# A two-layer diffusion backbone on one core: the last third of a modulation matrix-vector product moves from the gMLP stage to the mixer's output projection

## The chip, the core and the metric

The program runs on 1 core of one Trainium2 chip. The metric is the device time of one execution in microseconds (us). TensorE (PE) multiplies matrices into PSUM, VectorE (DVE), ScalarE (ACT) and GpSimd (POOL) work element by element, and SyncE (SP) issues the DMAs, in program order: a DMA whose buffer is not free holds back those behind it on SP.

## The reference

The model has an even layer (gMLP beside a bidirectional long convolution, "Hyena") and an odd one (attention). Each layer has a SwiGLU feed-forward part, and each sub-layer is modulated by six vectors per layer, which come from one product with a conditioning vector:

```python
def adaln(cond, w_mod, b_mod):
    return jnp.split(jax.nn.silu(cond) @ w_mod + b_mod, 6, axis=-1)

sh1, sc1, g1, sh2, sc2, g2 = adaln(c[:, None, :], mod_w[layer], mod_b[layer])
h = modulate(x, norm1_g[layer], sh1, sc1)
y = gmlp_hyena_mixer(h, ...)          # even layer; ends with concatenate([y_a, z]) @ w_out
x = x + g1 * y
x = x + g2 * swiglu(modulate(x, norm2_g[layer], sh2, sc2), ffn_w_gu[layer], ffn_w_down[layer])
```

There are 512 latent and 256 context tokens (six tiles of 128), and 1024 features; `mod_w` is 1024 by 6144 for each layer. Everything is float32.

## The kernel before

**Stages.** `build` runs the filters of the convolution, then the gMLP stage (`gmlp`), the convolutions (`hyena`), the mixer's output projection (`mix_out`), the first feed-forward part, attention and the second feed-forward part. A tile scheduler sets the order on every engine from the order of the code, priorities and its own estimates; a matmul with 3-way split operands (`mm3`, and `prod` in `project_tm`) is three matmuls, high by high, low by high, high by low.

**Weight loads and fill steps.** Every block of weights goes through `wload` (L158): a DMA of 512 KB into a tile `raw`, a rounding copy to `whi` on ACT (L166), and the remainder `wlo` on DVE (L167). `load_y` (L700) does the same with the mixer's activations, from `yu` (gMLP) and `yz` (convolution) in DRAM, 384 KB each. All of them, and the modulation too, share three `raw` buffers: a new `raw` can be loaded when an earlier one has been read for the last time.

Before each load, `wload` and `load_y` call `fill`, which takes `nfill` (or one) steps from a generator `self.filler`. The generator is `adaln` (L320): for a layer and one of three groups of 2048 columns it makes 16 steps; a step loads 512 KB of `mod_w` into a `raw` and multiplies it by the conditioning columns `sc` in four matmul instructions (eight records in the trace), straight from `raw`, into one PSUM tile `pa`. A 17th step adds the bias, transposes the result and stores it to `moddr`. The pool `pa` has one buffer, and the long convolutions use it as well, for the sums of their inverse transforms (L771). Group 1 holds the gate of the mixer and the shift of the feed-forward part, group 2 its scale and gate; group 2 is first needed by the norm ahead of the feed-forward part.

**gMLP stage.** `gmlp` has 16 weight loads (eight in two `project_tm`, eight in four `wcols`). `nfill` is 2 there, so the 32 loading steps of groups 1 and 2 all stand in this stage; the scheduler starts the first of them while the filters still run. `fill(99)` at L238 takes what is left.

**Mixer's output projection.** `mix_out` (L910) multiplies 16 blocks of 128 activations rows (eight `yu`, eight `yz`) by `even_w_out`, in two halves of the columns, `cg` 0 and 1. A half has eight weight loads; a block of one load is 36 matmuls (six token tiles, two rows of blocks, three products). In half 0 the blocks 0 to 3 use `yu`, which `hyena` has loaded before the last convolutions; the blocks 4 to 7 each load two `yz` tiles first. The tokens' old values `xr` (six DMAs of 512 KB) and the gates (two) are loaded here too. Blocks of half 0 run in between the matmuls of the last two convolutions, which are a chain over PE, DVE, POOL and ACT. The last convolution's result is stored by L800, on SP.

Of the kernel before, what the change touches and what calls it, by code (L numbers as in the profile page):

```python
# [113 lines left out]
class Builder:  # L114
# [93 lines left out]
    def build(self, upto=99):  # L208
        nc, tc = self.nc, self.tc
        with ExitStack() as es:  # L210
            self.base = es.enter_context(self.pool("base"))

            edge = es.enter_context(self.pool("edge", "right"))
            edge.tile([P, EDGE // 4], F32, tag="edge", name="edge", bufs=1)
            self.dr = es.enter_context(tc.tile_pool(name="dr", bufs=1, space=bass.MemoryType.DRAM))
            es.enter_context(self.weights(3, 3, 3))
            e1 = es.enter_context(ExitStack())
            with ExitStack() as e2:
                hp = e2.enter_context(self.pool("hT0", "right"))
                with self.psum(), self.pool("filt") as fp, self.pool("filtc") as fc:  # L220
                    with tc.high_priority(offset=2 * HF):
                        self.consts()
                        self.conditioning()
                        self.filter_hidden(fp)
                    self.prologue()
                    with self.pool("xin", "right") as xp:
                        self.filter_spectra(fc, xp, hp)
                if upto <= 3:
                    return
                e1.enter_context(self.psum())  # L230
                self.filler = self.adaln_steps([(0, 1), (0, 2)])
                with self.pool("gmlp") as gp:
                    self.nfill = 2
                    self.gmlp(gp)
                    self.nfill = 1
                pg0 = e2.enter_context(self.pool("pages0", "right"))
                with self.pool("pages1", "right") as pg, self.pool("conv") as cp:
                    self.fill(99)  # L238
                    self.load_dft(pg)
                    ysu = self.hyena(cp, (pg0, pg), hp)  # L240
                if upto <= 4:
                    return
                self.fill(99)
                xp = es.enter_context(self.pool("xres"))
                xs = [self.t(xp, [P, D], F32, "xr", TT) for _ in range(TT)]
                self.sp = es.enter_context(self.pool("norm"))
                with self.pool("mix") as m2, self.pool("ysz") as mp:
                    self.mix_out(m2, mp, pg0, xs, ysu)
            if upto <= 6:
                return  # L250
            e3 = es.enter_context(ExitStack())
            with self.pool("hT", "right") as hp:
                self.filler = self.adaln_steps([(1, 0), (1, 1), (1, 2)])
                self.ffn(hp, xs, 0)
                self.fill(99)
                if upto <= 7:
                    return
                kvp = e3.enter_context(self.pool("attkv"))
                kv = self.attention_in(hp, kvp, xs)
            e1.close()  # L260
            with self.pool("atts") as ap:
                self.attention(ap, xs[0:4], *kv)
                if upto <= 8:
                    return
            e3.close()
            es.enter_context(self.psum())
            hp = es.enter_context(self.pool("hT2", "right"))
            self.ffn(hp, xs[0:4], 1)
# [913 lines left out]
```

## Time and profile before

| | us |
|---|---|
| median of 3 runs | 2102.85 |
| lowest and highest | 2101.89, 2104.19 |
| the profiled execution | 2103.87 |
| its span in the trace | 2102.1 |
| PE busy in the span | 2006.0 |
| DVE, ACT, POOL busy | 1136.0, 674.4, 281.6 |

The trace is of one execution. "Busy" adds up the records of an engine; idle time in front of an instruction is put down to the engine or DMA that ended it. The granted clock of PE is a share of full speed: 1.00 is 2.4 GHz and half of it the lower level, 1.2 GHz; a mean between the two is a stretch with both.

### The profile page before, as it was taken

What the parts mean: (1) busy time and instruction counts of PE and PEld (TensorE: products, weight loads), DVE (VectorE), ACT (ScalarE), POOL (GpSimd) and SP (SyncE); (2) the same over time, 40 slices, a digit from 0 to 9 for tenths busy, and PEclk for the clock granted to TensorE, in tenths of its full rate; (3) what the DMA queues carried; (4) which work ended last, traced back from release to release, by engine and by line L of the source; (5) the groups of instructions that cost most, each with busy time, mean ns of one, the idle gap of its engine ahead of it and who ended that gap; (6) DMA issues with size and microseconds to landing.
All of it is one profiled execution on the core that took longest, in us unless ns stands there. A gap on an engine that the chain in (4) does not pass through costs nothing.

```text
span 2102.1 us, 28261 instructions
## 1 busy us (share of the span) xinstructions
PE 2006.0 (95%) x11259; PEld 1721.0 (82%) x11259; DVE 1136.0 (54%) x1963; ACT 674.4 (32%) x1234; POOL 281.6 (13%) x267
## 2 busy tenths in 40 slices
PE   5899999999999899899999999998989989999997
PEld 2667878899999788698888888997869978888886
DVE  5876173577787742533333333356677654444447
ACT  4654122333323321511111111213567642222222
POOL 3464000012121210200000000003150020000001
PEclk9999999999999999899999999999999999999999
DMA  7764345522322352333334343221220023233331
GB/s 255 226 213 149 107 152 175 184 78 70 100 83 72 124 203 68 111 91 106 119 107 122 120 121 101 61 69 58 64 80 1 31 71 91 81 110 100 90 106 65
DMA packets 207181, 227.82 MB, mean 108 GB/s; under 512 B 8569, under 2 KB 173546, under 8 KB 206794
## 3 DMA queue, kind: packets, MB, share of 16 engines
q1 hardware_dynamic: 206576, 219.95, 33.5%
q0 software_dynamic: 288, 5.90, 0.7%
q8 instruction: 89, 1.46, 0.3%
q14 instruction: 42, 0.34, 0.1%
q10 hardware_dynamic: 186, 0.17, 0.0%
HBM read 204.91 MB, written 21.07 MB: 108 GB/s over the span
## 4 chain that ended last, share of the span: by engine, by line
PE 88%; DMA 5%; DVE 3%; issue 1%; ACT 1%; POOL 1%; SPq 0%; DVEq 0%; POOLq 0%; ACTq 0%
PE pp L144 16%; PE pp L148 15%; PE pp L146 15%; PE pc L980 13%; PE pp L815 11%; PE pc L815 4%; PE pa L332 2%; DMA raw<-in_mod_w 2%; PE pc L144 1%; PE pc L146 1%; PE pc L148 1%; PE pa L148 1%; PE pa L146 1%; PE pa L144 1%; PE pt L1031 1%
## 5 line engine op out<-in xcount | busy, mean ns | idle before, releaser
L166 ACT CAST whi<-raw 128x1024 fp32r<-128x1024 f32 x208 | 216.7, 1052 | 881.0 <-PE pp L146 279.5
L167 DVE TENSOR_TENSOR wlo<-raw,whi 128x1024 fp32r<-128x1024 f32 x208 | 260.4, 1260 | 374.4 <-ACT whi L166 370.8
L144 PE MATMUL pp<-hTh,whi 128*128 128x384 f32 (+2 forms) x1088 | 324.9, 351 | 1.2 <-ACT whi L166 1.2
L146 PE MATMUL pp<-hTl,whi 128*128 128x384 f32 (+2 forms) x1088 | 324.0, 349 | 0.0
L148 PE MATMUL pp<-hTh,wlo 128*128 128x384 f32 (+2 forms) x1088 | 323.2, 350 | 0.0
L984 DVE TENSOR_TENSOR fy<-pc,fy 128x512 f32<-128x512 f32 x180 | 120.8, 689 | 192.3 <-PE pc L980 192.1
L144 PEld LDWEIGHTS pp<-hTh,whi 128*128 128x128 f32 x1088 | 198.9, 189 | 24.5 <-ACT fa L965 4.9
L148 PEld LDWEIGHTS pp<-hTh,wlo 128*128 128x128 f32 x1088 | 200.0, 189 | 17.2 <-DVE wlo L167 2.1
L146 PEld LDWEIGHTS pp<-hTl,whi 128*128 128x128 f32 x1088 | 199.8, 189 | 12.6
L980 PE MATMUL pc<-whi,fasl 128*128 128x512 f32 x440 | 172.3, 392 | 0.2 <-DVE fasl L155 0.2
L980 PE MATMUL pc<-wlo,fash 128*128 128x512 f32 x440 | 172.2, 391 | 0.0
L908 POOL TENSOR_TENSOR xr<-xr,nh 128x512 f32<-128x512 f32 x35 | 49.1, 1428 | 909.8 <-DVE nh L907 905.7
L980 PE MATMUL pc<-whi,fash 128*128 128x512 f32 x440 | 166.4, 394 | 0.0
L144 PE MATMUL pp<-hT,whi 128*128 128x512 f32 (+1 forms) x512 | 135.7, 341 | 1.3 <-ACT whi L166 1.3
L146 PE MATMUL pp<-hT,whi 128*128 128x512 f32 (+1 forms) x512 | 136.6, 341 | 0.0
L148 PE MATMUL pp<-hT,wlo 128*128 128x512 f32 (+1 forms) x512 | 134.5, 340 | 0.0
L980 PEld LDWEIGHTS pc<-whi,fash 128*128 128x128 f32 x440 | 81.9, 188 | 22.0 <-issue 5.4
L980 PEld LDWEIGHTS pc<-wlo,fash 128*128 128x128 f32 x440 | 82.6, 188 | 17.5
L980 PEld LDWEIGHTS pc<-whi,fasl 128*128 128x128 f32 x440 | 82.6, 188 | 16.3 <-DVE fasl L155 0.6
L144 PEld LDWEIGHTS pp<-hT,whi 128*128 128x128 f32 x512 | 79.5, 189 | 13.6 <-ACT whi L166 1.8
L146 PEld LDWEIGHTS pp<-hT,whi 128*128 128x128 f32 x512 | 80.2, 189 | 10.9
L148 PEld LDWEIGHTS pp<-hT,wlo 128*128 128x128 f32 x512 | 79.7, 188 | 11.5 <-issue 1.2
(344 smaller groups left out, 3794.8 us busy)
## 6 DMA issues: line engine op xcount, KB each, us to landing
raw<-in_mod_w SPq DMA_DIRECT2D x96, 512.0 KB
raw<-in_ffn_w_gu SPq DMA_DIRECT2D x88, 512.0 KB
raw<-in_ffn_w_down SPq DMA_DIRECT2D x44, 512.0 KB
raw<-in_even_w_in SPq DMA_DIRECT2D x40, 512.0 KB
G<-G SPq DMA_DIRECT2D x48, 256.0 KB
Gc<-G SPq DMA_DIRECT2D x16, 768.0 KB
raw<-in_even_w_out SPq DMA_DIRECT2D x16, 512.0 KB
dec<-in_k_dec SPq DMA_DIRECT2D x48, 128.0 KB
```

The lines of the kernel that those rows point to most:

```text
L144: mm(o, lh, rh, start=start, stop=False)
L146: mm(o, lh, rl, start=False, stop=False)
L148: mm(o, ll, rh, start=False, stop=stop)
L166: self.nc.scalar.copy(hi, raw)
L167: self.nc.vector.tensor_sub(lo, raw, hi.bitcast(F32))
L332: nc.tensor.matmul(ps[32 * j:32 * j + 32, hs], self.sc[:, k, :], raw[:, j, :], start=k == 0, stop=k == KT - 1, tile_position=(0, 32 * j))
L815: self.nc.tensor.matmul(ps, x[:, ts], y[:, a, :], start=k + a == 0 and i == 0, stop=k + a == wk - 1 and i == 2)
L908: (eng or nc.gpsimd).tensor_add(x[:, cs], x[:, cs], tmp)
L980: nc.tensor.matmul(ps, x[:, ts], y[:, 0, cs], start=i == 0 and j == 0, stop=i == 1 and j == 2)
L984: nc.vector.tensor_add(ys[q][:, cs], ps, ys[q][:, cs])
L1031: self.nc.tensor.transpose(ps[:, js], src[:, js], self.eye)
```

## The change

The generator for the gMLP stage holds group 1 alone and gives one step per weight load. Group 2 gets a generator of its own in `mix_out`, which is drained when `mix_out` ends; `fill` in `wload` and `load_y` takes one step from it per load, so 16 of the 24 loads of `mix_out` have a loading step ahead of them, and one has the closing step.

```diff
-                self.filler = self.adaln_steps([(0, 1), (0, 2)])
+                self.filler = self.adaln_steps([(0, 1)])
                 with self.pool("gmlp") as gp:
-                    self.nfill = 2
                     self.gmlp(gp)
-                    self.nfill = 1
...
-                self.fill(99)
                 xp = es.enter_context(self.pool("xres"))
...
                 with self.pool("mix") as m2, self.pool("ysz") as mp:
+                    self.filler = self.adaln_steps([(0, 2)])
                     self.mix_out(m2, mp, pg0, xs, ysu)
+                    self.fill(99)
```

The lines of the file move up by one from here on (L814 is the old L815, L331 the old L332). In the rows below a number behind a name tells instances apart: `raw_7736` is one load, and its high part is `whi_7738`; `hT_...` are the loaded `yu`, `page` and `ysz` the loaded `yz`.

SP, from the last load of `yu` to the gates of `mix_out`. Before:

```order
L705 DMA raw_7090<-yu_660_2380 128x768
L163 DMA raw_7736<-in_even_w_out 128x2x512
L163 DMA raw_7778<-in_even_w_out 128x2x512
L163 DMA raw_7820<-in_even_w_out 128x2x512
L163 DMA raw_7862<-in_even_w_out 128x2x512
L715 DMA Gc_7540<-G_25_116 128x1536
L163 DMA raw_7904<-in_even_w_out 128x2x512
L705 DMA raw_7910<-yz_662_2382 128x768
L705 DMA raw_7917<-yz_663_2383 128x768
L163 DMA raw_7954<-in_even_w_out 128x2x512
L800 DMA yz_668_2388<-zf_7342 128x768
```

SP, the same place, after:

```order
L704 DMA raw_6979<-yu_660_2380 128x768
L329 DMA raw_7626<-in_mod_w 128x4x256
L163 DMA raw_7632<-in_even_w_out 128x2x512
L329 DMA raw_7674<-in_mod_w 128x4x256
L714 DMA Gc_7429<-G_25_116 128x1536
L163 DMA raw_7680<-in_even_w_out 128x2x512
L329 DMA raw_7722<-in_mod_w 128x4x256
L799 DMA yz_668_2388<-zf_7231 128x768
L799 DMA yz_669_2389<-zf_7529 128x768
L163 DMA raw_7728<-in_even_w_out 128x2x512
L329 DMA raw_7770<-in_mod_w 128x4x256
```

Ahead of the store of the second last convolution there were six weight loads and two of `yz`; now there are two weight loads and three of `mod_w`, and the third weight load stands behind the store of the last convolution (`yz_669`) too.

PE, the end of the last convolution (`pa`) and what follows it. Before:

```order
L148 MATMUL pa_7668<-kd_3752,Yi1l_7665 128x128
L815 MATMUL pp_7733<-whi_7864,hT_7061 128x512
L815 MATMUL pp_7733<-wlo_7865,hT_7060 128x512
L815 MATMUL pc_7734<-whi_7864,hT_7060 128x512
L815 MATMUL pc_7734<-whi_7864,hT_7061 128x512
```

PE, the same place, after:

```order
L148 MATMUL pa_7557<-kd_3641,Yi1l_7554 128x128
L331 MATMUL pa_7625<-raw_7626,sc_92 32x256 x4
L331 MATMUL pa_7625<-raw_7674,sc_92 32x256 x4
L331 MATMUL pa_7625<-raw_7722,sc_92 32x256 x4
L814 MATMUL pp_7619<-whi_7730,hT_6947 128x512
L814 MATMUL pp_7619<-whi_7730,hT_6948 128x512
```

Before, PE goes on with the fourth weight block (`whi_7864`); after, it takes the first three steps of group 2, and then the third block (`whi_7730`, the load `raw_7728`).

SP, in the blocks of half 0 that load `yz`. Before:

```order
L705 DMA raw_8010<-yz_666_2386 128x768
L800 DMA yz_669_2389<-zf_7640 128x768
L898 DMA gate_1595_7726<-moddr_8_99 128x1024
L898 DMA gate_1596_7728<-moddr_8_99 128x1024
L928 DMA xr_7695<-in_x 128x1024
L928 DMA xr_7696<-in_x 128x1024
L705 DMA raw_8017<-yz_667_2387 128x768
L928 DMA xr_7697<-in_x 128x1024
L163 DMA raw_8054<-in_even_w_out 128x2x512
```

SP, the same blocks, after:

```order
L329 DMA raw_7886<-in_mod_w 128x4x256
L163 DMA raw_7892<-in_even_w_out 128x2x512
L329 DMA raw_7898<-in_mod_w 128x4x256
L704 DMA raw_7904<-yz_664_2384 128x768
L329 DMA raw_7911<-in_mod_w 128x4x256
L704 DMA raw_7917<-yz_665_2385 128x768
L329 DMA raw_7954<-in_mod_w 128x4x256
L163 DMA raw_7960<-in_even_w_out 128x2x512
```

A block there took three loads through the `raw` buffers and now takes six, every other one a step of group 2.

## Rows read from the trace of the kernel before

**Rows 1.** The page's busy time of the engines in the whole span, with the share of the span and the number of instructions.

```profile
PE 2006.0 (95%) x11259; PEld 1721.0 (82%) x11259; DVE 1136.0 (54%) x1963; ACT 674.4 (32%) x1234; POOL 281.6 (13%) x267
```

**Rows 2.** Busy time by stretch (from:to, length, busy us and instructions of each engine, granted clock, DMA share, GB/s): the gMLP stage, two stretches of the last convolutions, the rest of half 0, half 1, and the start of the feed-forward part.

```profile
195.00:284.00 89.00, 84.64 (x418) 66.53 (x417) 26.07 (x45) 18.41 (x28) 2.17 (x4) 0.96 0.35 113
284.00:420.00 136.00, 134.66 (x906) 115.02 (x906) 73.14 (x108) 34.10 (x51) 6.92 (x9) 1.00 0.54 182
...
691.49:735.66 44.17, 38.06 (x217) 33.67 (x217) 31.17 (x61) 11.66 (x21) 10.96 (x9) 0.88 0.31 105
735.66:753.06 17.40, 17.40 (x96) 15.04 (x95) 10.97 (x17) 6.32 (x9) 4.60 (x4) 1.00 0.30 91
753.06:789.15 36.09, 36.09 (x161) 29.87 (x161) 13.89 (x18) 8.64 (x11) 5.36 (x5) 1.00 0.73 252
789.15:854.43 65.28, 65.28 (x290) 53.78 (x291) 18.36 (x28) 12.91 (x17) 11.37 (x11) 1.00 0.21 63
...
857.00:910.00 53.00, 44.72 (x265) 39.89 (x264) 24.56 (x48) 24.46 (x48) 1.96 (x3) 0.87 0.42 130
```

**Rows 3.** What PE waited for, of the filters' last 75 us (first two rows) and of the gMLP stage (the others): us in total, times, longest.

```profile
PE pa L332 <- DMA raw<-in_mod_w: 2.7, 2, 2.0
...
PE pp L815 <- DVE G L636: 2.3, 1, 2.3
PE pa L332 <- DMA raw<-in_mod_w: 2.1, 1, 2.1
...
PE pp L144 <- ACT whi L166: 1.3, 1, 1.3
```

**Rows 4.** The chain that ended last (start, us, what), where it runs over three steps of the modulation in one piece; 24 records are three steps.

```profile
331.80 1.43 PE pa L332 x24
```

**Rows 5.** The chain at the gMLP stage's start, where DVE waits for a store of `G` (start, us, what), and PE's timeline there.

```profile
203.86 4.55 DMA G<-G
...
204.78 0.28 PE L148 MATMUL pp<-hfsh,kf 128*128 128x256 f32 x1
207.12 0.64 PE L332 MATMUL pa<-raw,sc 128*32 128x256 f32 x8 [2.06 <-DMA raw<-in_mod_w]
210.06 1.19 PE L815 MATMUL pp<-whi,hT 128*128 128x512 f32 x2 [2.29 <-DVE G L636]
211.05 0.63 PE L815 MATMUL pp<-wlo,hT 128*128 128x512 f32 x1
211.47 1.05 PE L815 MATMUL pp<-whi,hT 128*128 128x512 f32 x2
```

**Rows 6.** Busy time of L815 alone (the mixer's matmuls) by stretch: PE busy, with the records in brackets (one that straddles a border counts in both), weight loads, granted clock, DMA share, GB/s.

```profile
691.49:735.66 44.17, 18.79 (x73) 14.05 (x73) 0.88 0.31 105
735.66:753.06 17.40, 13.73 (x58) 10.63 (x59) 1.00 0.30 91
753.06:789.15 36.09, 36.09 (x159) 29.87 (x160) 1.00 0.73 252
789.15:854.43 65.28, 65.28 (x288) 53.70 (x287) 1.00 0.21 63
```

**Rows 7.** Timelines of the last convolution (start, us, engine, line, idle before): its last `Yi0l` on DVE; PE's last matmuls of the first sum and of the second; ACT's and DVE's reading of the second sum; SP's store of the result.

```profile
740.16 0.75 DVE L155 TENSOR_TENSOR Yi0l<-T,Yi0h 128x512 fp32r<-128x512 f32 x1 [0.41 <-ACT Yi0h L154]
...
745.05 0.28 PE L148 MATMUL pa<-kd,Yi0l 128*128 128x256 f32 x1
...
752.95 0.28 PE L148 MATMUL pa<-kd,Yi1l 128*128 128x128 f32 x1
...
753.32 0.27 ACT L781 COPY B<-pa 128x128 f32<-128x128 f32 x1 [4.74 <-PE pa L148]
...
753.82 0.28 DVE L785 TENSOR_TENSOR s<-pa,B 128x128 f32<-128x128 f32 x1
...
754.65 0.32 SPq L800 DMA_DIRECT2D yz<-zf  x1
```

**Rows 8.** Timelines of ACT at the first two weight blocks of the mixer, and of PE at the first.

```profile
692.18 1.04 ACT L166 CAST whi<-raw 128x1024 fp32r<-128x1024 f32 x1 [0.72 <-DMA raw<-in_even_w_out]
...
698.76 1.05 ACT L166 CAST whi<-raw 128x1024 fp32r<-128x1024 f32 x1 [0.86 <-DMA raw<-in_even_w_out]
...
693.28 2.93 PE L815 MATMUL pp<-whi,hT 128*128 128x512 f32 x6 [1.79 <-ACT whi L166]
```

**Rows 9.** The chain ahead of the first feed-forward part, where it runs over loads of `mod_w` from issue to landing (start, us, what).

```profile
856.63 3.60 DMA raw<-in_mod_w
...
864.76 5.97 DMA raw<-in_mod_w
871.91 4.46 DMA raw<-in_mod_w
```

**Rows 10.** One load of `yz`: SP's issue of the first of two, and ACT's cast that waited for it.

```profile
743.72 3.52 SPq L705 DMA_DIRECT2D raw<-yz  x2
...
746.79 0.84 ACT L707 CAST page<-raw 128x768 fp32r<-128x768 f32 x1 [0.99 <-DMA raw<-yz]
```

**Rows 11.** The tile `raw` from 680 to 860 us: what reads it (ns min/median/max).

```profile
L166 ACT CAST whi<-raw x18: 1037/1054/1057, 692.2 to 853.2; 128x1024 fp32r<-128x1024 f32 x18
L167 DVE TENSOR_TENSOR wlo<-raw,whi x18: 1214/1225/2380, 695.9 to 854.3; 128x1024 fp32r<-128x1024 f32 x18
...
L707 ACT CAST ysz<-raw x5: 832/835/835, 757.3 to 775.1; 128x768 fp32r<-128x768 f32 x5
L708 DVE TENSOR_TENSOR ysz<-raw,ysz x5: 951/959/960, 758.5 to 776.0; 128x768 fp32r<-128x768 f32 x5
```

## The prediction

> **What bounds the kernel now.** I read the engines' busy time first: PE is busy 95% of the span [rows 1], so time is saved only by taking matmuls or PE's waits away, and lost by making PE wait. Then the stages that the change touches, by stretch [rows 2]. The gMLP stage has 4.4 us of PE idle time in 89.0 (195 to 284) and 1.3 in 136.0 (284 to 420). Of the mixer's output projection, the stretch to 735.66 has 6.1 us idle in 44.17; the last 17.40 us of the convolutions, the rest of half 0 (36.09) and half 1 (65.28) have no idle time at all, at full clock. So the place that gives work up has few waits, and the place that receives it has none: what counts is whether it stays so. The waits themselves are the next view [rows 3]: 2.7 us for `mod_w` in the filters, 2.1 for `mod_w`, 2.3 for DVE and 1.3 for a weight block in the gMLP stage.
>
> **The moved work itself: 0.** Three steps take 1.43 us of PE in one piece [rows 4], so a step is 0.48 and the 16 steps are 7.6 us. They leave the filters and the gMLP stage and come back in `mix_out`, where no PE time is free for them: net nothing. The 16 loads of 512 KB move along. The closing step (bias loads, transposes, stores to `moddr`) is moved too; on SP it stands in half 1, with three of its weight blocks loaded ahead, and I cost it at nothing; uncovered it would be one load's time, 4 to 6 us [rows 9].
>
> **Removed waits: -3.0 us.** With one step per load the gMLP stage asks for half the `mod_w`. Of the waits of [rows 3] the one of 2.7, and the 1.3 for a weight block, can go, 4.0 in all. The pair around 207 I leave: the chain there is a store of `G` of 4.55 us that DVE waits for, and PE idles 2.06 and 2.29 in its course [rows 5]; the steps only fill that gap. I take 3.0 of the 4.0, as a load may still land late in the filters. Bounds 0 and -6.4: the lower one has all 4.0 and the 2.4 that the low clock behind the gap costs (twelve matmuls of L815 take 5.1 us from 210.06 instead of 12 x 0.2267 = 2.7; 0.2267 is 65.28 us by 288 records in [rows 6]).
>
> **A. The convolutions' tail: +3.5 us.** `pa` has one buffer, which the convolutions' sums hold, so no step of group 2 can run before the last sum has been read. But their loads are issued earlier, and the order of SP shows three `mod_w` tiles among the first loads; of three `raw` buffers they keep two and then all. So only two weight blocks get through instead of nearly four: 72 mixer matmuls to hide the convolution chain behind, where there were 73 + 58 - 1 = 130 [rows 6]. 58 x 0.2267 = 13.2 us of cover are gone. If the chain were the bound already, PE would idle for all of it: +13.2; if the chain gets faster by as much, since its matmuls no longer queue behind mixer matmuls, 0. Nearer to which? For the last order (17.40 us, PE never idle) I add up the chain alone, from 735.66: 5.25 us to the end of the last `Yi0l` at 740.91; the first sum's matmuls behind it, which ended at 745.33, 4.42 later with mixer matmuls among them, and for which I take 3.05 without; 1.3 until `pa` has been read and can hold the second sum; 1.35 for that sum's last twelve matmuls: 11.0 us [rows 7]. The 3.05, the 1.3 (0.96 as in B, and a wait for PE to take up) and the 1.35 are estimates. PE's work left there is the convolution's 3.67 (17.40 - 13.73) with some transposes, 4.25, and 24 mixer matmuls, 5.4: 9.7. So 1.3 us idle. In the stretch before, the first weight block is now the second load on SP behind a `mod_w`, so its cast comes later, between 692.18 and 698.76 as the second's did [rows 8]; PE waited 1.79 us for the first already, and I take 2.2 more. 1.3 + 2.2 = 3.5.
>
> **B. The gap behind the last convolution: +8.3 us.** The third weight block stands on SP behind the store of the last convolution, and needs a `raw` that the first step gives free only when `pa` has been read. Before, PE went straight on. Now: ACT's copy to DVE's sum takes `pa` away at 754.10, about 0.96 us behind the last matmul, and the store is issued at 754.65 [rows 7]. Then the weight load is issued some 2.0 us behind the last matmul, lands after 4.46 (the middle one of 3.60, 4.46 and 5.97, all loads of the same 512 KB [rows 9]) and is cast in 1.05 [rows 11]: `whi` is ready 7.4 us after the last matmul. PE has three steps, to 0.96 + 1.43 = 2.4. It idles 0.96 + 5.0 = 5.96. Behind the idle stretch of [rows 5] the next twelve matmuls ran at the low clock, 2.4 us longer; I add that here: 8.3. Bounds 5 (landing in 3.60, clock kept) and 10 (5.97).
>
> **C. The ring of `raw` buffers: +8.5 us.** Blocks 4 to 7 of half 0 each took three loads; now six: three `mod_w`, one weight block, two `yz`. PE's work for a block is 36 x 0.2267 + 3 x 0.48 = 9.6 us, and by it alone four blocks take 38.4. A buffer is held from issue to last reading. Per block with a landing of 4.46 (a `yz` took 3.07 from issue to cast, alone [rows 10]; I take 3.9 in a crowd): three steps 3 x (4.46 + 0.48), a weight block 4.46 + 1.05 + 1.23 = 6.74, two `yz` 2 x (3.9 + 0.83 + 0.96) [rows 11]; sum 32.9 by three buffers = 11.0 us a block. With 3.60 and 3.07 it is 27.8 / 3 = 9.3, under PE's 9.6, and costs nothing; with 5.97 for all it is 41.6 / 3 = 13.9, or 4 x 4.3 = +17. SP also issues strictly in order and PE consumes in order, so buffers idle: walking SP's order row by row with landings of 4.0 I get blocks of 11.6, 12.9, 11.0 and 11.4, together 46.9, 8.5 over 38.4. DMA capacity doesn't bind, with a share of 0.73 in that stretch before [rows 2]. The `xr` and gate loads come with blocks 2 and 3 of half 0, whose weights are by then in SBUF, and I give them nothing extra; half 1 has none of the 16 steps (four go with the blocks 0 to 3, twelve with 4 to 7), and one load for each 8.2 us of PE work, so a load of 6 us stays hidden: 0.
>
> **Sum:** -3.0 + 3.5 + 8.3 + 8.5 = +17.3 on the profiled execution's 2103.87 gives 2121.2; the median lies 1.0 below that execution, so 2120.
>
> The Trainium skill, "Perfetto Trace Analysis", section "Identifying Performance Opportunities", says that consistent gaps on the engine that should be saturated can mean that SBUF has no space for the next tile. It speaks against the change: before, no such gap shows in 753 to 854, and term C says that six loads in three buffers make some.
>
> **Rivals.**
> 1. *The ring keeps up* (C = 0): landings of 3.60 or less, as the shortest of [rows 9], and `yz` in 3.07. Then -3.0 + 3.5 + 7.4 = +8, 2111. For it: one load of the three; against it: the other two, and that more loads are now in flight. 17%. The Trainium skill, "DMA: Bandwidth & Descriptors", section "Anatomy of one DMA", gives a fit for loads that GpSimd issues, about 2.0 us plus the bytes at 436 GB/s, that is an estimated 3.2 us for 512 KB; with it C would be nothing. The trace's loads, issued by SP, took 3.60 to 5.97, and I go by those.
> 2. *The clock falls in the ring.* The stretch from 857 to 910, 44.72 busy of 53.00, had a mean granted clock of 0.87, against 1.00 where PE never waited [rows 2]. Should PE's gaps of C lower it, a block at the low level is 36 x 0.42 = 15.1 us plus the steps' 1.4, 16.5, against 11.7 above: +4.8 each. For three of four blocks +14: 2134. Speaks against it: gaps of 1 to 3 us in 12 are small. 20%.
> 3. *Small costs only:* A and C nothing, B 5.0, the waits -4.0: +1, 2104. It needs short landings and a convolution chain that shrinks with its cover. 10%.
> 4. *Faster.* The waits of the filters and the gMLP stage go with the low-clock stretch (-6.4), and A to C come to nothing since the steps fill the chain's gaps: 2096 to 2098. Decided by whether the third weight block lands before PE has done the three steps; by the order of SP it can't be issued so early unless the store of the last convolution is. 5%.
>
> That the change doesn't do what it says is excluded: the order shows the steps in `mix_out`. The forecast has 48%.
>
> **How the numbers follow.** The range goes from rival 3 (A and C at 0) to rival 2 with all four blocks low (2139): 2104 to 2140. Outside lie rival 4, half of rival 3, and A at 13.2 or C at 17 together with a low clock; under 2 in 10. 0.2% is 4.2 us, about what this kernel's measurement can tell from no change: faster than 2098.6 has rival 4's 5%; within it lie rival 3 and a little of rival 1, 11%; slower 84%.
>
> **What the profile of the changed kernel would show.** Two weight blocks (72 matmuls of L814) before the last convolution ends, and PE idle there a few us more than before (A). Behind it three steps of L331 in one piece, then a wait of about 5 us for `whi`, and a granted clock below 1.00 (B). Waits of L331 and L814 for `raw`, `whi` and `page` in half 0, with blocks of some 11.7 us instead of 9.6 (C). Half 1 at 65.3 us, and nothing changed from the feed-forward part on. The filters and the gMLP stage shorter by 7.6 + 3. I'm wrong if PE hardly waits in half 0 (rival 1), if its clock is well below 1.00 there (rival 2), or if the tail of the convolutions loses more than a few us.

## The result and the profile after

| | before | after |
|---|---|---|
| median (us) | 2103.52 (4 runs) | 2125.69 (4 runs) |
| lowest and highest | 2101.89, 2108.67 | 2122.00, 2127.64 |
| ratio to before, 95% interval | | 1.0101 [1.0081, 1.0121] |
| span of the profiled execution | 2102.1 | 2123.6 |

The changed kernel is slower by 1.0%. The page's busy time, as in [rows 1], hardly moves:

```profile
PE 2013.4 (95%) x11259; PEld 1725.1 (81%) x11259; DVE 1135.2 (53%) x1963; ACT 675.1 (32%) x1234; POOL 277.5 (13%) x267
```

PE's busy time rises by 7.4 us, with the same number of instructions; the other 14 us of the 21.5 by which the span grows are idle time. The same point of the program in both timelines shows where it goes: the table has the start of a PE instruction before and after.

| point of the program (start, us) | before | after | difference |
|---|---|---|---|
| last inverse-filter matmul of the filters (L148 `hfsh,kf`) | 204.78 | 200.03 | -4.8 |
| last gMLP matmul (L148 `wsh,vsl`) | 338.81 | 327.00 | -11.8 |
| first `X1h` of the convolutions | 401.05 | 385.92 | -15.1 |
| last matmul of the last convolution (L148 `kd,Yi1l`) | 752.95 | 728.75 | -24.2 |
| last mixer matmul (L815, now L814, `wlo,ysz`) | 854.04 | 875.25 | +21.2 |
| first transpose of the feed-forward part's norm | 854.91 | 876.13 | +21.2 |

So up to the first `X1h`, where the steps are gone, the program is 15.1 us shorter, and the mixer's output projection alone loses all that was gained and 21 more. Its stretches, as in [rows 2] (from:to, length, busy us and instructions of PE, PEld, DVE, ACT, POOL, granted clock, DMA share, GB/s): the last two convolutions in two pieces, the gap and the weight blocks 2 and 3, the blocks 4 to 7 one by one, half 1, and the start of the feed-forward part. (The first stretch begins some 3 us earlier in the program than the 691.49 of [rows 2].)

```profile
673.00:717.57 44.57, 35.48 (x208) 32.09 (x207) 30.69 (x68) 10.67 (x20) 9.95 (x9) 0.85 0.28 93
717.57:728.98 11.41, 10.01 (x62) 8.74 (x60) 6.51 (x13) 2.43 (x5) 4.58 (x4) 1.00 0.00 0
728.98:755.55 26.57, 21.89 (x105) 16.19 (x104) 4.69 (x7) 3.41 (x4) 0.00 (x0) 0.81 0.81 292
755.55:768.10 12.55, 10.36 (x61) 7.18 (x60) 3.07 (x3) 2.71 (x3) 0.00 (x0) 1.00 0.72 231
768.10:785.07 16.97, 13.84 (x69) 9.20 (x68) 2.27 (x4) 2.71 (x3) 0.00 (x0) 0.80 0.55 187
785.07:797.55 12.48, 10.68 (x60) 7.00 (x60) 2.86 (x3) 1.83 (x3) 0.00 (x0) 1.00 0.60 195
797.55:809.71 12.16, 9.85 (x54) 7.11 (x53) 6.03 (x7) 3.59 (x4) 0.90 (x2) 1.00 0.65 216
809.71:875.60 65.89, 65.89 (x295) 54.35 (x294) 21.63 (x35) 14.09 (x18) 18.27 (x15) 1.00 0.27 86
878.00:931.00 53.00, 44.73 (x267) 39.57 (x266) 24.55 (x48) 24.43 (x48) 2.16 (x3) 0.87 0.43 130
```

Half 1 (65.89 us) and the feed-forward part are as before but for the closing step, 0.6 us in half 1. All idle time of the output projection lies ahead of 809.71. What PE waited for from 728 to 812 (us in total, times, longest), none of which stood in the same place before:

```profile
PE pp L814 <- ACT page L706: 4.9, 2, 3.1
PE pp L814 <- ACT whi L166: 3.7, 1, 3.7
PE pp L814 <- ACT ysz L706: 2.9, 3, 1.2
PE pa L331 <- DMA raw<-in_mod_w: 1.5, 2, 1.2
PE pa L331 <- ACT B L780: 1.0, 1, 1.0
```

PE's timeline behind the last convolution (start, us, idle before in brackets):

```profile
730.00 2.61 PE L331 MATMUL pa<-raw,sc 128*32 128x256 f32 x24 [0.98 <-ACT B L780]
736.31 3.78 PE L814 MATMUL pp<-whi,hT 128*128 128x512 f32 x8 [3.70 <-ACT whi L166]
739.89 1.37 PE L814 MATMUL pc<-whi,hT 128*128 128x512 f32 x4
741.19 0.64 PE L331 MATMUL pa<-raw,sc 128*32 128x256 f32 x8
```

Three steps, held until `pa` is read, then a wait for the weight block. The steps take 2.61 us instead of the 1.43 of [rows 4], and the next twelve matmuls 4.88 instead of 2.72: the low clock level (the stretch from 728.98 to 755.55 has a mean granted clock of 0.81).

**The sum**, by the terms of the prediction and at its price of 0.48 us a step. A (tail): from -15.1 to -24.2 is 9.1 us less, with 58 mixer matmuls fewer (72 records of L814 ahead of 728.98, where there were 130), 13.1 us: 4.0 lost. B (gap): 0.98 + 3.70 idle, 1.2 + 2.2 low clock, 8.1. C (blocks 4 to 7): 54.2 us from 755.55 to 809.71, against the 38.4 of the prediction, 15.8. The relief before: 15.1 with the 7.6 us of steps in it, 7.5. Of the 16 steps four stand ahead of 755.55 and cost what was reckoned. 4.0 + 8.1 + 15.8 - 7.5 = 20.4; with the closing step in half 1, 0.6, that is 21.0 of the 21.2 at the norm.

### The profile page after: what moved, and what is told of

Read it like the earlier page. It is cut to its first block, busy times and chain, and to the rows that moved or that the text cites. A ratio compares the mean times of both kernels' runs of the same rounds, so it can differ in the third digit from the quotient of the medians.

```text
span 2123.6 us, 28270 instructions
## 1 busy us (share of the span) xinstructions
PE 2013.4 (95%) x11259; PEld 1725.1 (81%) x11259; DVE 1135.2 (53%) x1963; ACT 675.1 (32%) x1234; POOL 277.5 (13%) x267
## 4 chain that ended last, share of the span: by engine, by line
PE 87%; DMA 5%; DVE 3%; issue 1%; ACT 1%; POOL 1%; SPq 0%; DVEq 0%; POOLq 0%; ACTq 0%
PE pp L144 16%; PE pp L148 15%; PE pp L146 15%; PE pc L979 13%; PE pp L814 10%; PE pc L814 3%; DMA raw<-in_mod_w 2%; PE pa L331 2%; PE pc L146 1%; PE pc L148 1%; PE pc L144 1%; PE pa L146 1%; PE pa L144 1%; PE pa L148 1%; PE pt L1030 1%
## 5 line engine op out<-in xcount | busy, mean ns | idle before, releaser
L148 PE MATMUL pp<-hTh,wlo 128*128 128x384 f32 (+2 forms) x1088 | 323.9, 350 | 0.0
L148 PEld LDWEIGHTS pp<-hTh,wlo 128*128 128x128 f32 x1088 | 199.9, 189 | 17.0 <-DVE wlo L167 1.6
L148 PE MATMUL pp<-hT,wlo 128*128 128x512 f32 (+1 forms) x512 | 134.5, 339 | 0.0
L814 PE MATMUL pp<-whi,hT 128*128 128x512 f32 x256 | 81.6, 406 | 7.1 <-ACT whi L166 3.7
```

Source lines behind the costliest of these rows:

```text
L148: mm(o, ll, rh, start=False, stop=stop)
L814: self.nc.tensor.matmul(ps, x[:, ts], y[:, a, :], start=k + a == 0 and i == 0, stop=k + a == wk - 1 and i == 2)
```

## The experiments

There are three theories for the mixer's output projection. **Sharing:** a loaded step holds one of three `raw` buffers, and with it the loads behind it, until PE comes to it. **PE:** the steps' own matmuls cost more than 0.48 us each. **Traffic:** the loads as such are too many, or collide with others (`xr`). Ratios are to runs of the kernel before on the same chip.

### Without the steps, and without their loads

`no_steps` keeps two steps and the closing step, and `no_loads` keeps all, both on one tile of zeros:

```diff
-            for k in range(KT):
+            for k in range(1 if (l, g) == (0, 2) else KT):      # no_steps alone
...
+                if (l, g) == (0, 2):
+                    raw = self.still
+                else:
...
```

> Leaves out 14 of the 16 loading steps of group 2 in the mixer's output projection, their loads as well as their matmuls (two remain, on a tile of zeros, with the closing step); what is moved out of the filters and the gMLP stage stays out. By the traces the program without group 2 is 15.1 us shorter at the start of the last blocks, and has the cover of 130 mixer matmuls again: about 2103.5 - 15.1 + 1.5 (two steps and closing) = 2090. The PE theory (relief of only 16 x 0.48 plus 3.0, as predicted) expects 2094; 2100 or more would say that the tail loses time for another reason than the steps.

> Keeps the matmuls of all 16 loading steps of group 2 where they are, but on one tile of zeros, so that their 16 loads are left out and the raw buffers hold weights and yz alone. Ring theory (the loss is the loads' passage through three buffers and SP): no wait of PE in half 0, two weight blocks ahead of the last convolution become four again, and the time is that of no_steps plus 14 steps of PE work: 14 x 0.48 = 6.7 us (2097) if a step costs what three in a row cost, or 14 x 0.78 = 10.9 us (2101) if a step between other matmuls costs more. Rival (the loss is the steps' matmuls on PE, or pa): the time stays above 2115.

Measured: no_steps 2090.65 us, 0.9930 [0.9908, 0.9952]; no_loads 2098.99, 0.9966 [0.9950, 0.9981]. So the PE theory is out as the main cause, though a step does cost more than 0.48 us. Both runs fit the sharing theory and the traffic theory alike, since neither run has the loads; the runs further down tell these two apart. In no_loads PE never waits from the last convolution to the end of half 1 (its two stretches there):

```profile
741.40:760.00 18.60, 18.60 (x140) 12.92 (x139) 6.05 (x9) 4.68 (x7) 0.00 (x0) 1.00 0.90 325
760.00:853.00 93.00, 93.00 (x445) 73.94 (x443) 27.54 (x41) 17.27 (x21) 17.44 (x16) 1.00 0.25 78
```

From the last convolution to the last mixer matmul no_loads loses 10.0 us on the kernel before and no_steps 1.8: 14 steps are 8.2 us, 0.59 each, with seven of the 16 in one piece. In the change the same stretch loses 45.4 us (from -24.2 to +21.2), of which 13.1 are mixer matmuls that moved behind the last convolution; of the other 32.3 the steps' matmuls explain some 10, and the rest comes with their loads.

### A later start

`late` starts the generator with the first `yz` load:

```diff
-                    self.filler = self.adaln_steps([(0, 2)])
...
                 while k >= len(ys):
+                    if len(ys) == 8:
+                        self.filler = self.adaln_steps([(0, 2)])
```

> The generator of group 2 starts only with the first yz load, so no step's load is ahead of the weight blocks 0 to 3: twelve steps in the blocks 4 to 7 of half 0, four in half 1. If the tail (about 4 us) and the gap behind the last convolution (about 8 us) come from the steps' raws that wait for pa, both go: 2125.7 - 12 = 2113 to 2114, with the waits for raw, yz and mod_w in the blocks 4 to 7 as before. If these blocks set the end by themselves (the ring starts earlier, but is as slow), 2120 or more. If the ring only suffered from its late start, below 2108.

Measured: 2121.92 us, 1.0078 [1.0055, 1.0101]. Tail and gap are gone, as expected: the last convolution ends 15.8 us earlier than before with a relief of 14.9 ahead of it, and PE goes on without a wait. But the time falls by some 4 to 5 us and not by 12: from there to the last mixer matmul it loses 31.3 us, 21 more than the 10.0 of no_loads. PE's timeline has two long waits, where `xr` and the gates are loaded and the `raw` ring starts:

```profile
756.83 1.08 PE L330 MATMUL pa<-raw,sc 128*32 128x256 f32 x8 [6.12 <-DMA raw<-in_mod_w]
762.47 2.07 PE L813 MATMUL pp<-whi,page 128*128 128x512 f32 x4 [4.56 <-ACT page L705]
```

So A and B are what the steps ahead of the weight blocks cost, but some 7 of the 12 us come back in the blocks 4 to 7. I read that as the ring starting without a lead over PE; what the loads of `xr` have in it is the next question.

### Without the tokens' loads

`no_xr`, and the same in the late version, `late_no_xr`:

```diff
-                    nc.sync.dma_start(xs[i], src)
+                    nc.gpsimd.memset(xs[i], 0.0)
```

In the trace after, the weight blocks 3 and 4 come late. SP's issues (start, us; `mod_w` issues between left out), and ACT's casts of the two blocks:

```profile
734.48 0.38 SPq L163 DMA_DIRECT2D raw<-in_even_w_out  x1
735.21 2.51 SPq L927 DMA_DIRECT2D xr<-in_x  x4
737.77 1.29 SPq L927 DMA_DIRECT2D xr<-in_ctx  x2
...
741.89 0.38 SPq L163 DMA_DIRECT2D raw<-in_even_w_out  x1
...
754.71 0.34 SPq L704 DMA_DIRECT2D raw<-yz  x1
```

```profile
741.81 1.05 ACT L166 CAST whi<-raw 128x1024 fp32r<-128x1024 f32 x1 [5.55 <-DMA raw<-in_even_w_out]
752.37 1.05 ACT L166 CAST whi<-raw 128x1024 fp32r<-128x1024 f32 x1 [9.51 <-DMA raw<-in_even_w_out]
```

> The changed kernel without the six loads of the tokens' old values xr (they are set to zero by GpSimd instead, which leaves 3 MB of transfers out). In the trace after, the two weight blocks issued beside them take 7.3 and 10.5 us from issue to cast, and the ring of the blocks 4 to 7 starts only then. Theory that my working left these loads out wrongly: the two weight blocks come in 4 to 5 us, the ring starts 4 to 6 us earlier, and the time falls by 3 to 6 us, to about 2121. Rival (the ring is held by PE's order alone): no change within 1 us.

> The version with the late start (from the first yz load), without the six xr loads (xr set to zero by GpSimd). In that version PE waits 6.1 us for mod_w and 4.6 for yz between 750 and 763, just where the xr and gate loads run with a DMA share of 0.87. If it is their traffic: about 10 us less, 2111. If it is the ring: within 2 us of 2121.9.

Measured: no_xr 2119.71 us, 1.0065 [1.0042, 1.0089], against 1.0101 for the change; late_no_xr 2117.53, 1.0037 [1.0018, 1.0056], against 1.0078. The intervals of each pair overlap a little, so the times alone leave it just open; the profiles agree with them. From the last convolution to the last mixer matmul no_xr loses 39.6 us instead of 45.4, and late_no_xr 27.4 instead of 31.3. (The second is neither of the two outcomes expected, 10 us or within 2.) In no_xr the second cast comes 3.6 us behind the issue instead of 10.5 (the issue was at 742.65):

```profile
746.26 1.05 ACT L166 CAST whi<-raw 128x1024 fp32r<-128x1024 f32 x1 [2.40 <-DMA raw<-in_even_w_out]
```

The first of the two is not sooner (7.6 us, against 7.3), so `xr` isn't what delays that one; nothing tried here says what is. In late_no_xr the wait of 6.12 shrinks to 1.35, and that of 4.56 stays (4.70). The traffic of `xr` is some 4 to 6 us of the loss, by making the ring start late, as the second cast shows; the larger part stays without it.

### Buffers of their own

`after_own3` is the change with three separate buffers, in the mixer's pool, for the loads of group 2:

```diff
-                raw = self.t(self.wp, [P, 4, 256], F32, "raw", self.wbufs[0])
+                raw = self.t(self.m2, [P, 4, 256], F32, "mraw", 3) if (l, g) == (0, 2) else self.t(self.wp, ...)
```

> The changed kernel, but the loads of group 2 get three buffers of their own in the mixer's pool instead of sharing the three raw buffers with the weights and yz; all 16 steps stay in the mixer's output projection. Theory (the loss is the sharing: a loaded step holds a raw until PE comes to it in order, and the weight block behind it can't be issued): no wait of PE for weights, yz or mod_w from the last convolution on; the blocks cost 16 steps x 0.62 us (9.9 us, as without loads) and the closing step; a ratio of about 0.9975 to before, 2098 for a before of 2103.5. Rival (too many loads for SP or the DMA engines, or loads of mod_w that wait for their own buffer hold the weight blocks back on SP just the same): a ratio of 1.004 or more.

Measured: 2105.29 us, 0.9991 [0.9976, 1.0007]. The loads are all there, and PE has no wait from 737 us to the end of the output projection, as two of its stretches show; the DMA share is higher than in any of the change's stretches above:

```profile
737.00:760.00 23.00, 23.00 (x123) 17.60 (x122) 7.49 (x11) 4.77 (x6) 0.00 (x0) 1.00 0.87 280
760.00:780.00 20.00, 20.00 (x104) 14.84 (x103) 7.06 (x8) 3.77 (x4) 3.67 (x3) 1.00 0.96 337
```

So in this version neither the loads, nor SP, nor the traffic makes PE wait. It differs from the change in one more thing. The pool's memory is free only when the convolutions are done, so the steps start later: six stand in half 0, which ends at 781.33, and ten in half 1, where the change has none. Half 0 with as many steps as in the change and buffers of their own was not tried; the same number of loads per block, with and without buffers of their own, is compared in half 1 below. The time is 3 us above what was expected: from the last convolution to the last mixer matmul 13.1 us are lost without a wait at full clock. Less 0.6 for the closing step that is 0.78 for each of the 16 steps, which here stand singly between mixer matmuls. The trace after shows the same price:

```profile
780.88 0.63 PE L814 MATMUL pc<-whi,ysz 128*128 128x512 f32 x2
781.44 0.64 PE L331 MATMUL pa<-raw,sc 128*32 128x256 f32 x8
782.01 0.50 PE L814 MATMUL pp<-whi,ysz 128*128 128x512 f32 x1
782.35 0.40 PE L814 MATMUL pp<-wlo,ysz 128*128 128x512 f32 x1
```

From 780.88 to 782.35 three mixer matmuls need 0.68; the step has taken 0.79.

### Half 1 alone

`half1` puts group 2 into half 1, three steps per weight load; `half1_own4` is the same with four buffers of their own; `half1_2` shares the `raw` buffers again, with two steps per load:

```diff
         for cg in range(2):
+            if cg == 1:
+                self.filler, self.nfill = self.adaln_steps([(0, 2)]), 3      # half1_2: 2
```

> Group 2 in half 1 alone, three steps per weight load there, where a load has 8.2 us of matmuls to itself. Ring theory: four loads per block need 3 x (4.46 + 0.48) + 6.74 = 21.6 us of three buffers, 7.2 a block, under the 9.6 us of PE work, so nothing waits; the tail and the gap go, and the time is 2103.5 - 15.1 + 16 steps at 0.48 to 0.78 (7.7 to 12.5) + 0.6 for the closing step = 2097 to 2101.5, faster than before by 2 to 6 us. Rival: that the closing step comes too late for the norm of the feed-forward part, or that loads of mod_w hold back the weight blocks: 2105 or more.

Measured: 2119.78 us, 1.0071 [1.0051, 1.0092], some 18 us or more above what was expected: my reckoning by throughput (a block's loads divided by three buffers) failed. PE's timeline has a wait of 4 to 5 us in every second block (the first here), and SP's shows why:

```profile
773.21 1.50 PE L331 MATMUL pa<-raw,sc 128*32 128x256 f32 x24
779.65 3.78 PE L814 MATMUL pp<-whi,hT 128*128 128x512 f32 x8 [4.95 <-ACT whi L166]
785.03 0.64 PE L331 MATMUL pa<-raw,sc 128*32 128x256 f32 x8
```

```profile
755.00 5.80 SPq L329 DMA_DIRECT2D raw<-in_mod_w  x3
773.91 0.37 SPq L163 DMA_DIRECT2D raw<-in_even_w_out  x1
```

The three steps are issued by 760.80 and then fill all three buffers until PE, in its order, has done the block before; the weight block behind them is issued when the first step has been read, at 773.91. The loads aren't too slow: PE takes the steps without a wait, so their data lay ready in all three buffers while the weight block couldn't be issued.

> The version with group 2 in half 1 (three steps per weight load), with four buffers of its own for the steps' loads. In the version with shared buffers PE waits 4 to 5 us for a weight block at 779.65, 806.42 and 833.22, each time behind three steps in a row. Theory: those waits go, and with them the low clock behind them; 20 us less, a ratio of about 0.997 to before. Rival (four loads per block are too many for the DMA engines, whoever owns the buffer): the waits stay and the ratio is 1.006 or more.

Measured: 2100.49 us, 0.9972 [0.9959, 0.9984]: faster than before, and the best version here. Not one wait is left in the four stretches from 737 to 830; two of them:

```profile
760.00:780.00 20.00, 20.00 (x107) 15.77 (x106) 8.56 (x10) 3.15 (x3) 10.27 (x6) 1.00 0.79 258
780.00:805.00 25.00, 25.00 (x148) 18.88 (x150) 2.45 (x2) 2.28 (x3) 0.04 (x1) 1.00 0.67 227
```

From the last convolution to the last mixer matmul it loses 9.7 us: (9.7 - 0.6) / 16 = 0.57 for a step in a row of three, against 0.78 singly. A block has the same four loads here as in half1, so what half1 lost came from the three buffers that its steps held, and not from the loads. Buffers of their own are also more buffers, seven in all; seven shared ones were not tried.

> The version with group 2 in half 1, the three raw buffers shared as in the change, but with two steps per weight load instead of three, so that the steps are spread over all eight loads. Order theory: with three steps per load the three loaded steps fill all three buffers and PE comes to them only behind the block before, so the weight block is issued 4 to 5 us too late (773.21 the steps, 773.91 the issue, 779.65 the first matmul); with two per load the third buffer is the weight block's, it is loaded a block ahead, and no wait of PE for a weight block remains before the tail, at the same number of loads in all and no new buffer. Time: a ratio of 0.997 to 0.999 to before, the later closing step included. Rival (throughput: the loads of a block through three buffers take longer than PE's work): waits of PE remain in each block, and the ratio is 1.003 or more.

Measured: 2108.44 us, 1.0014 [1.0004, 1.0024]. In the first six blocks the order theory is right: with the third buffer left to the weight block nothing waits, with the same three shared buffers and as many loads in all (three in a block, where half1 had four).

```profile
775.00:805.00 30.00, 30.00 (x165) 22.73 (x164) 5.21 (x6) 2.11 (x2) 6.59 (x6) 1.00 0.46 155
805.00:835.00 30.00, 30.00 (x166) 22.69 (x165) 3.67 (x3) 3.66 (x4) 0.00 (x0) 1.00 0.47 159
```

But the time is above what was expected. The last two steps wait in the tail, the closing step comes later than I allowed for, and PE then waits 5.45 us for the norm of the feed-forward part, where it waited 0.60 before:

```profile
840.95 0.64 PE L331 MATMUL pa<-raw,sc 128*32 128x256 f32 x8 [0.49 <-DMA raw<-in_mod_w]
846.10 0.64 PE L331 MATMUL pa<-raw,sc 128*32 128x256 f32 x8 [2.02 <-DMA raw<-in_mod_w]
...
865.14 1.97 PE L384 MATMUL pp<-eye,nxn 128*128 128x128 f32 x8 [5.45 <-DVE nxn L379]
```

DVE's order in this trace shows what the norm waited for: the sums that end the output projection (`nh<-pp,gate`) stand behind the closing step's `modr` (849.68) and behind the `wlo` of the feed-forward part's first weight block (854.88), and start at 856.03, where in half1_own4 they start at 838.85. Which of the two holds them back wasn't tried by itself.

## Why the prediction was right, and where its sizes were off

The forecast was 2120 us, in a range of 2104 to 2140, slower; measured 2125.69. The case was the forecast's own, and none of the rivals. That the sum came within 4 us owes something to luck: what was gained ahead of the convolutions was 4.5 us more than forecast, and C 7.3 us more, and the two errors pull against each other.

- **The moved work, net 0:** right as a net to about 1 us, but the price wasn't 0.48. That is a step's share of three in one piece; in a row of three between other matmuls it was 0.57 (half1_own4), singly 0.78 (after_own3). What the steps cost where they came from stands in the busy time of their line alone (PE and PEld, granted clock, DMA share, GB/s), before and after; each pair of stretches takes in all steps ahead of the convolutions:

```profile
0.00:195.00 195.00, 19.11 (x208) 5.08 (x208) 0.96 0.66 215
195.00:425.00 230.00, 13.42 (x176) 4.62 (x176) 0.99 0.46 151
0.00:190.00 190.00, 15.13 (x168) 3.95 (x168) 0.96 0.63 207
190.00:410.00 220.00, 7.42 (x88) 2.40 (x88) 0.99 0.39 132
```

  128 records fewer, 16 steps, are 10.0 us less: 0.62 a step. Where they went, four cost some 1.9 us and twelve 9.3: 11.2.
- **Removed waits, -3.0:** the shortening was 15.1 us. Less the steps' 10.0 that is 5.1, more than 3.0 and inside the bound of -6.4. PE's idle time up to the first `X1h` fell from 43.8 to 40.2 us, so 3.6 of it are waits; the other 1.5 (low clock, closing step) weren't told apart. The store of `G` is still waited for, as I said; the wait is now 3.5 us in one (before: 2.06 and 2.29 [rows 5]):

```profile
PE pp L814 <- DVE G L635: 3.5, 1, 3.5
```

  This term isn't settled to the microsecond: in the nine further traces, whose code is the same up to there (but for one memset in two of them), the first `X1h` came 10.3 to 16.9 us earlier than before.
- **A, +3.5:** measured 4.0, with the 72 matmuls as named; the last order took 11.41 us with 1.4 idle (reckoned 11.0 and 1.3). Shown by late and after_own3, in which it is gone.
- **B, +8.3:** measured 8.1: idle 0.98 and 3.70 (reckoned 0.96 and 5.0), low clock 3.4 (reckoned 2.4). Gone in the same two versions. Two slips in its working are small: in [rows 7] 754.10 lies 0.87 us behind the end of the last matmul, not 0.96, and 2.0 + 4.46 + 1.05 is 7.5, not 7.4.
- **C, +8.5: the mis-sized term.** It measured 15.8: 9.4 idle, 2.8 low clock (thirteen matmuls from 772.32 to 778.04 took 5.7 us instead of 2.9), and 3.6 for twelve steps that cost 0.78 and not 0.48. The walk along SP's order gave 8.5 us of idle time, and that the 9.4 are so near is luck. "The `xr` and gate loads [...] I give them nothing extra" failed: without `xr` the same four blocks take 48.6 us, at full clock and with 5.6 us idle (no_xr, 756.33 to 804.98), instead of 54.2. So the walk was 3 us too high for the loads that it had in it, and had left out the price of `xr`. A price per block by dividing buffer time by three is a lower bound only: half1 lost 20 us where this gave nothing, as loaded buffers stood behind PE's order. (One sum of the working is wrong: with 5.97 for all a block's buffers take 43.1 us and not 41.6, which makes the upper end +19 and not +17.)
- **Rival 1** (the ring keeps up) is out by the waits; **rival 2** (the clock) shows in one block of four, 2.8 us, not in three; **rivals 3 and 4** needed A to C near nothing.

The rule of the Trainium skill, "Perfetto Trace Analysis", section "Identifying Performance Opportunities", that consistent gaps can mean too little space for the next tile, agrees with these runs: 9.4 us of gaps in the blocks 4 to 7 of the change, and none in half 1 with buffers of their own (half1_own4), where half1 has three of 4 to 5 us. They also show a gap without a lack of space, since half1_2 has none with the buffers that make half1 wait; there it is the order.

## What to carry to other kernels

Work that is put in between to fill gaps takes the buffers and the queue of the loads that it is put between: ask which buffer each step holds, from its issue until the engine comes to it in order, and which load is behind it. Throughput alone doesn't tell this; as long as filler held all three shared buffers PE waited, with two of three it didn't, and with buffers of its own neither. I would carry this on as a rule for n buffers, at most n - 1 of them for the filler, but only three were tried. And filler belongs where each load has time to spare: here that was half 1 with four separate buffers, 0.3% faster than before.

## What was not expected of the hardware

A step's price changed with its neighbours: 1.43 us for three in one piece (0.48), 0.57 a step in rows of three between mixer matmuls, 0.78 singly, all at full clock; the mixer matmul behind a step took 0.34 us to the next start, instead of 0.23. Why is not shown. And a weight load of 512 KB took 10.5 us from issue to cast with 3 MB of the tokens' loads issued ahead of it, and 3.6 us at the same place without them; the weight load just ahead of it took 7.3 and 7.6 us either way.
